# Splitting the later weights of an encoder layer early, storing q and k as rows of three parts, and reading one branch from where it was made

## The chip, the cores and the metric

One core of a Trainium2 chip runs the whole layer. The metric is device time in microseconds (us) of one execution. A NeuronCore has five engines, each with an in-order stream of instructions: TensorE (PE, matrix products; PEld is its weight load), VectorE (DVE), ScalarE (ACT), GpSimd (POOL) and SyncE (SP), which here issues nearly all transfers (DMAs). They meet only at semaphores.

## The reference, cut to what matters

```
h = rmsnorm(x, norm_g)                                   # x: 1024 tokens x 1024
q, k, v, glu_a, glu_b, pool_in, sgu_u, sgu_v, gates = split(h @ w_in)   # 8 pieces of 256, gates 1024
y_a = neighborhood_attention(q, k, v, na_rpb)            # 8 heads of 32, windows of 8 rows x 16 columns
y_b = silu(layernorm(depthwise_conv31(glu_a * sigmoid(glu_b)))) @ conv_pw
y_c = pool_scale * grouped_linear(multiscale_mean(pool_in) - pool_in)
y_d = gelu(sgu_u) * (sgu_w applied per chunk of 128 to layernorm(gelu(sgu_v)) + sgu_b)
y   = concat(y_a, y_b, y_c, y_d) * silu(gates)
out = rmsnorm(x + y @ w_out, final_g)
```

All inputs are float32. A big product is made from parts: each operand is split into `hi` (rounded to PE's float32r) and `lo = x - hi`, and three products hi*hi, lo*hi and hi*lo are added in one PSUM bank.

## The kernel before

**Stages.** First h is normalised and split into `hhi` and `hlo` (128 channels x 8 x 1024 tokens), while v and sgu_v are projected (L213, until about 55 us). Then comes the middle stage: the other 20 blocks of 128 output channels, in the order of the list `work`. Items 0 to 3 feed the convolution (glu_b, glu_a twice), 4 and 5 are q and k of the first four heads, 6 and 7 the pooling, 8 and 9 sgu_u, 10 and 11 q and k of the other heads, 12 to 19 the eight gate blocks, for the branch blocks 6, 7, 4, 5, 0, 2, 3, 1 of the concatenation (0 and 1 attention, 2 and 3 convolution, 4 and 5 pooling, 6 and 7 spatial gating). An item is two *banks* (512 tokens each) of 24 matmuls (L371), so there are 40 banks. Last come two halves of the output projection (L822, L856) with the residual and the final norm.

**Weights.** `prep` loads item n+1 (512 KB) when item n begins; ACT rounds each half to `whi` (L354), and `wlo` is made by POOL in two pieces per half for items 0 to 8 (L360), by DVE for items 9 to 19 (L356). `wraw` has two buffers, `whi` and `wlo` three each.

**What runs beside it.** Each bank ends with its `evac_*` function on ACT and DVE. Between banks generators are advanced: `conv_steps` (97 steps, 92 taps on DVE, L584) over banks 4 to 22; `att_steps` (18 steps, from bank 18 to 37), each with scores on PE (L475 to L478), bias and maximum on DVE, a reduction over partitions on POOL (L488), exponentials on ACT and the product with v on PE (L516, sums by L520); and `conv_norm` (5 steps, banks 23 to 27): mean (L612), variance on PE (L622), two small trips through DRAM (`s_d`, L626 to L634) that end in the row `rb`, then swish (L637 to L644) and the pointwise product (L651). After the fourth and the last group of heads the sums of the exponentials also make a trip through DRAM (`o_d`, `r_d`, L526 to L539).

**Through DRAM.** q and k are written to DRAM in parts hi and lo, and gathered per head into `kst` (hi, lo, hi, a mask) and `qst` (hi, hi, lo, a mask), three DMAs of 32 partitions and one for the mask each time. The spatial gating result `ut` goes to `yd_d` and comes back to `yr` when its gate block begins (L675, L722), as pooling does through `yc_d`.

**Order.** The program is written in this order, and a scheduler then sets the order on each engine from its own estimate of times. z banks for the items: two PSUM buffers.

Of the kernel before, what the change touches and what calls it, by code (L numbers as in the profile page):

```python
# [16 lines left out]
P = 128  # L17
D = 1024
# [28 lines left out]
POOL_W = 9  # L47

ATT0, ATT1, CONV0, CONV1 = 18, 37, 4, 22
# [9 lines left out]
def encoder_kernel(ctx: ExitStack, tc: tile.TileContext, a: dict, out: bass.AP):  # L59
# [273 lines left out]
    yr = {kt: slot("yr") for kt in (6, 7, 4, 5)}  # L333
    sq = [slot("sq") for _ in range(2)]
    yb = [slot("yb") for _ in range(2)]
# [11 lines left out]
    def prep(ct, eng):  # L347
        raw = wpool.tile([P, KO, P], F32, name="wraw")
        ld.dma_start(out=raw, in_=a["w_in"][ct])
        wts[ct] = []  # L350
        for q in range(2):
            hi = wpool.tile([P, 4, P], F32R, name="whi", bufs=3)
            lo = wpool.tile([P, 4, P], F32R, name="wlo", bufs=3)
            s.activation(out=hi, in_=raw[:, 4 * q:4 * q + 4], func=AF.Copy)  # L354
            if eng is v:
                v.tensor_tensor(out=lo, in0=raw[:, 4 * q:4 * q + 4], in1=hi, op=ALU.subtract)  # L356
# [20 lines left out]
    q_d = dram.tile([2, 2, 4, DH, S], F32, name="q_d")  # L377
    k_d = dram.tile([2, 2, 4, DH, SW], F32, name="k_d")
# [3 lines left out]
    def evac_q(hg):  # L382
        hi, lo = qkt[hg][0:2]

        def f(b, z):
# [42 lines left out]
    def att_loads(gi):  # L428
# [177 lines left out]
    def conv_norm():  # L606
        for b in range(2):
# [27 lines left out]
        yield  # L635
        for c in range(2):
            v.tensor_tensor(out=cc[c][:, 0:S], in0=cc[c][:, 0:S], in1=rb, op=ALU.mult)  # L637

        for c in range(2):
            t = sq[c][:, 0:S]  # L640
            s.activation(out=cc[c][:, 0:S], in_=cc[c][:, 0:S], func=AF.Identity, scale=cvec[:, 1, c:c + 1],
                         bias=cvec[:, 2, c:c + 1])
            s.activation(out=t, in_=cc[c][:, 0:S], func=AF.Tanh, scale=0.5)
            v.scalar_tensor_tensor(out=cc[c][:, 0:S], in0=t, scalar=1.0, in1=cc[c][:, 0:S], op0=ALU.add, op1=ALU.mult)  # L644
        yield
        for c in range(2):
            for b in range(2):
                sl = slice(b * 512, (b + 1) * 512)
                ps = bbank()
                for k in range(2):  # L650
                    pe.matmul(ps, lhsT=pw[:, k, c * P:(c + 1) * P], rhs=cc[k][:, sl], start=(k == 0), stop=(k == 1))  # L651
                s.activation(out=yb[c][:, 0:S].rearrange("p (n e) -> p n e", e=2)[:, :, b], in_=ps, func=AF.Copy, scale=0.5)
            yield


    yd_d = dram.tile([2, P, S], F32, name="yd_d")

    def evac_u(c):
        u = ut[c]

        def f(b, z):
# [12 lines left out]
            if b == 1:  # L674
                ld.dma_start(out=yd_d[c], in_=u[:, 0:S])  # L675
# [38 lines left out]
    y = {0: ya[0], 1: ya[1], 2: yb[0], 3: yb[1]}  # L714
    y.update(yr)

    def evac_g(kt, src):
        def f(b, z):
            br = y[kt]
            sl = slice(b * 512, (b + 1) * 512)  # L720
            if b == 0 and src is not None:
                ld.dma_start(out=br[:, 0:S], in_=src)  # L722
# [3 lines left out]
            if src is not None:  # L726
# [8 lines left out]
    for c in range(2):  # L735
# [3 lines left out]
    work += [(T_G + kt, evac_g(kt, src)) for kt, src in  # L739
             ((6, yd_d[0]), (7, yd_d[1]), (4, yc_d[0]), (5, yc_d[1]), (0, None), (2, None), (3, None), (1, None))]  # L740
# [4 lines left out]
    att, conv, norm = att_steps(), conv_steps(), conv_norm()  # L745
    prep(work[0][0], g)
    bank = 0
    for n, (ct, evac) in enumerate(work):
        if n + 1 < len(work):
            prep(work[n + 1][0], g if n + 1 < POOL_W else v)  # L750

        for b in ((1, 0) if n == 0 else (0, 1)):
# [4 lines left out]
            for gen, count, b0, b1 in ((att, 18, ATT0, ATT1), (conv, 97, CONV0, CONV1), (norm, 5, CONV1 + 1, CONV1 + 5)):  # L757
# [16 lines left out]
    def wo_pair(j, half, hi, lo):  # L774
        raw = wpool.tile([P, 2, 512], F32, name="wraw")
# [181 lines left out]
```

## Time and profile before

| | us |
|---|---|
| median of 3 runs | 436.57 (436.07 to 437.01) |
| profiled execution | 435.86 |
| its span, first to last instruction | 434.1 |
| PE busy in the span | 415.9 (96%) |
| DVE, ACT, POOL busy | 312.3, 184.8, 112.2 |
| mean granted PE clock | 0.985 of full speed |

The span is 1.76 us shorter than the execution's own time. PE is busy nearly all of it, so time can come only from the 18.2 us in which it is not, or from those in which it runs at a lower clock.

### The profile page before, as it was taken

What the parts mean: (1) busy time and instruction counts of PE and PEld (TensorE: products, weight loads), DVE (VectorE), ACT (ScalarE), POOL (GpSimd) and SP (SyncE); (2) the same over time, 40 slices, a digit from 0 to 9 for tenths busy, and PEclk for the clock granted to TensorE, in tenths of its full rate; (3) what the DMA queues carried; (4) which work ended last, traced back from release to release, by engine and by line L of the source; (5) the groups of instructions that cost most, each with busy time, mean ns of one, the idle gap of its engine ahead of it and who ended that gap; (6) DMA issues with size and microseconds to landing.
All of it is one profiled execution on the core that took longest, in us unless ns stands there. A gap on an engine that the chain in (4) does not pass through costs nothing.

```text
span 434.1 us, 5888 instructions
## 1 busy us (share of the span) xinstructions
PE 415.9 (96%) x2150; PEld 331.2 (76%) x2150; DVE 312.3 (72%) x540; ACT 184.8 (43%) x314; POOL 112.2 (26%) x90
## 2 busy tenths in 40 slices
PE   7899999999999999999978889999999999999994
PEld 6788878888888778777846647787787788888883
DVE  4798676888988799999798647997882580093332
ACT  6757655222232328334336733344342452254332
POOL 0763402322226821111111101221111243620000
PEclk9999999999999999999995999999999999999998
DMA  7995106311775124163893141522011384402222
GB/s 273 421 418 186 54 25 206 88 48 51 228 245 150 48 97 146 50 219 104 271 235 90 52 168 54 170 94 65 11 48 61 122 269 183 145 2 97 97 98 97
DMA packets 28294, 59.56 MB, mean 137 GB/s; under 512 B 3910, under 2 KB 13354, under 8 KB 28266
## 3 DMA queue, kind: packets, MB, share of 16 engines
q1 hardware_dynamic: 28122, 58.93, 40.9%
q8 instruction: 17, 0.28, 0.3%
q10 hardware_dynamic: 144, 0.26, 0.2%
q14 instruction: 11, 0.09, 0.1%
HBM read 46.71 MB, written 12.47 MB: 136 GB/s over the span
## 4 chain that ended last, share of the span: by engine, by line
PE 80%; DMA 9%; DVE 5%; SPq 2%; ACT 1%; issue 1%; POOL 1%; DVEq 0%; ACTq 0%; POOLq 0%
PE z_ps L371 45%; DMA yr<-yd_d 3%; PE sb L213 3%; PE z_ps L213 3%; PE sb L822 3%; PE sb L856 3%; PE z_ps L822 2%; PE b_ps L856 2%; PE z_ps L856 2%; DMA xT_sb<-in_xT_dram 2%; PE pv L516 2%; PE sa L822 1%; PE ac L213 1%; PE b_ps L822 1%; PE pv L822 1%; PE ac L822 1%
## 5 line engine op out<-in xcount | busy, mean ns | idle before, releaser
L371 PE MATMUL z_ps<-hhi,whi 128*128 128x512 f32 x320 | 90.0, 400 | 1.5 <-DVE yr L728 1.3
L371 PE MATMUL z_ps<-hlo,whi 128*128 128x512 f32 x320 | 89.6, 398 | 0.0
L371 PE MATMUL z_ps<-hhi,wlo 128*128 128x512 f32 x320 | 87.8, 395 | 0.0
L371 PEld LDWEIGHTS z_ps<-hhi,whi 128*128 128x128 f32 x320 | 59.3, 190 | 17.8 <-issue 3.0
L371 PEld LDWEIGHTS z_ps<-hlo,whi 128*128 128x128 f32 x320 | 60.3, 189 | 14.8 <-issue 2.5
L371 PEld LDWEIGHTS z_ps<-hhi,wlo 128*128 128x128 f32 x320 | 60.5, 190 | 13.8 <-issue 1.1
L488 POOL PARTITION_ALL_REDUCE R<-M x16 | 29.9, 1868 | 134.3 <-DVE M L509 128.9
L584 DVE SCALAR_TENSOR_TENSOR ac<-d,pk,ac 128x512 f32<-128x512 f32 x62 | 46.6, 751 | 2.6 <-ACT ac L596 0.9
L360 POOL TENSOR_TENSOR wlo<-wraw,whi 128x256 fp32r<-128x256 f32 x36 | 27.4, 784 | 68.6 <-ACT whi L354 68.6
L354 ACT ACTIVATE whi<-wraw 128x512 fp32r<-128x512 f32 x40 | 25.0, 627 | 33.3 <-PE z_ps L371 31.5
L500 ACT ACTIVATE T<-T 128x1280 f32<-128x1280 f32 x16 | 20.4, 1272 | 15.5 <-DVE T L499 15.5
L584 DVE SCALAR_TENSOR_TENSOR ac<-ch,dws,ac 128x512 f32<-128x512 f32 x30 | 22.6, 755 | 1.8 <-ACT ac L585 0.8
L831 ACT ACTIVATE jk<-res 128x512 f32<-128x512 f32 (+1 forms) x17 | 10.2, 604 | 26.6 <-DVE res L829 25.6
L356 DVE TENSOR_TENSOR wlo<-wraw,whi 128x512 fp32r<-128x512 f32 x22 | 16.8, 764 | 5.1 <-ACT whi L354 5.0
L781 POOL TENSOR_TENSOR wlo<-wraw,whi 128x512 fp32r<-128x512 f32 x8 | 12.1, 1524 | 31.7 <-ACT whi L780 18.9
L829 DVE SCALAR_TENSOR_TENSOR res<-sa,res 128x512 f32<-128x512 f32 x2 | 1.4, 686 | 22.6 <-PE sa L822 22.6
L725 ACT ACTIVATE sg<-z_ps 128x512 f32<-128x512 f32 x16 | 9.5, 596 | 15.5 <-PE z_ps L371 14.1
L499 DVE TENSOR_TENSOR T<-T,pv 128x768 f32<-128x768 f32 x16 | 15.2, 948 | 0.0
L483 DVE SCALAR_TENSOR_TENSOR T<-sb,bt 128x768 f32<-128x768 f32 x16 | 15.2, 948 | 0.0
L505 DVE TENSOR_TENSOR R<-T 128x512 f32<-128x512 f32 x16 | 13.2, 827 | 2.6 <-ACT T L500 2.6
L481 DVE SCALAR_TENSOR_TENSOR T<-sa,bt 128x512 f32<-128x512 f32 x16 | 11.0, 685 | 3.7 <-PE pv L516 2.4
L781 POOL TENSOR_TENSOR wl<-wraw,wh 128x512 fp32r<-128x512 f32 x8 | 10.2, 1294 | 11.3 <-ACT wh L780 11.3
(279 smaller groups left out, 821.6 us busy)
## 6 DMA issues: line engine op xcount, KB each, us to landing
wraw<-in_w_in_dram SPq DMA_DIRECT2D x20, 512.0 KB
res<-in_x_dram SPq DMA_DIRECT2D x8, 512.0 KB
wraw<-in_w_out_dram SPq DMA_DIRECT2D x8, 512.0 KB
out_dram<-res SPq DMA_DIRECT2D x15, 256.0 KB
kst<-k_d SPq DMA_DIRECT2D x24, 136.0 KB
xT_sb<-in_xT_dram SPq DMA_DIRECT2D x6, 512.0 KB
qst<-q_d SPq DMA_DIRECT2D x24, 128.0 KB
vk<-va_d SPq DMA_DIRECT2D x8, 256.0 KB
```

The lines of the kernel that those rows point to most:

```text
L213: pe.matmul(z, lhsT=ha[:, 2 * c + k, ts], rhs=wa[:, k, :], start=(c == 0 and n == 0 and k == 0), stop=(c == 3 and n == 2 and k == 1))
L354: s.activation(out=hi, in_=raw[:, 4 * q:4 * q + 4], func=AF.Copy)
L356: v.tensor_tensor(out=lo, in0=raw[:, 4 * q:4 * q + 4], in1=hi, op=ALU.subtract)
L360: g.tensor_tensor(out=lo[:, w:w + 2], in0=raw[:, 4 * q + w:4 * q + w + 2], in1=hi[:, w:w + 2], op=ALU.subtract)
L371: pe.matmul(z, lhsT=wa[:, k, :], rhs=ha[:, 4 * q + k, b * 512:(b + 1) * 512], start=(n == 0), stop=(n == 3 * KO - 1))
L483: v.scalar_tensor_tensor(out=T[:, :, 256:640], in0=sb[:, :, 0:384], scalar=DH ** -0.5, in1=mf, op0=ALU.mult, op1=ALU.add)
L488: g.partition_all_reduce(R.rearrange("p h x -> p (h x)"), M.rearrange("p h x -> p (h x)"), P, bass.bass_isa.ReduceOp.max)
L500: s.activation(out=T, in_=T, func=AF.Exp)
L584: v.scalar_tensor_tensor(out=ac, in0=src, scalar=w, in1=ac, op0=ALU.mult, op1=ALU.add)
L781: g.tensor_tensor(out=lo[q], in0=raw[:, q], in1=hi[q], op=ALU.subtract)
L822: pe.matmul(acc[t], lhsT=y_[kt][:, ts], rhs=w_[q], start=(j == 0 and q == 0 and n == 0), stop=(j == 3 and q == 1 and n == 2))
L856: pe.matmul(o[:, c0:c1], lhsT=y_[kt][:, ts], rhs=w_[j][:, q, c0:c1], start=(j == 0 and q == 0 and n == 0), stop=(j == 3 and q == 1 and n = ...
```

## The change

1. Items 9 to 19: their weights are loaded and split in banks 1 to 13 by a new generator `split_ahead` (ACT rounds, POOL subtracts, in the buffers that later hold the keys), and both parts are stored in DRAM (`w_d`). `prep` of these items then only loads: hi into `wraw`, lo in two halves into a `whi` and a `wlo` buffer. No `wlo` is made on DVE any more in the middle stage.
2. q and k lie in DRAM as three parts per channel, so that one DMA of 96 partitions fills `qst` or `kst`; the keys' mask rows are loaded once. q and k are each written with three DMAs, before with two.
3. The spatial gating result is gated in place in `ut`; `yd_d` is gone. Pooling's result is loaded two items ahead.
4. The convolution's taps end one bank earlier (21), and its norm has 13 steps over banks 22 to 33; `yb` shares the buffers `sq`.
5. Banks 25, 28, 31 and 34 use the PSUM bank `ac` of the convolution in place of one of the two z buffers. The first half block of w_out is loaded into a query buffer, and its lo part made by DVE.

```diff
-POOL_W = 9
-ATT0, ATT1, CONV0, CONV1 = 18, 37, 4, 22
+NOW = 9
+EARLY0, EARLY1 = 1, 13
+ATT0, ATT1, CONV0, CONV1, NORM1 = 18, 37, 4, 21, 33
...
+    def prep(n):
+        ct = work[n][0]
+        wts[ct] = []
+        raw = wpool.tile([P, KO, P], F32 if n < NOW else F32R, name="wraw")
+        if n < NOW:
+            ld.dma_start(out=raw, in_=a["w_in"][ct])
+        else:
+            ld.dma_start(out=raw.bitcast(F32), in_=w_d[n][0])
...
+            else:
+                hi = part
+                lo = wpool.tile([P, 4, P], F32R, name=("whi", "wlo")[q], bufs=3)
+                ld.dma_start(out=lo.bitcast(F32), in_=w_d[n][1][:, 4 * q:4 * q + 4])
...
+    def split_ahead():
+        for n in range(NOW, len(work)):
+            w_d[n] = [dram.tile([P, KO, P], F32, name=f"w_d{n}_{i}") for i in range(2)]
+            raw = at.tile([P, 1280], F32, name="T", bufs=3)[:, 0:D].rearrange("p (k c) -> p k c", k=KO)
+            hi, lo = (ktile(2 * (n % 2) + i)[:, 0:D].rearrange("p (k c) -> p k c", k=KO) for i in range(2))
+            ld.dma_start(out=raw, in_=a["w_in"][work[n][0]])
+            for q in range(2):
+                ks = slice(4 * q, 4 * q + 4)
+                s.activation(out=hi[:, ks], in_=raw[:, ks], func=AF.Copy)
+                low(lo[:, ks], raw[:, ks], hi[:, ks])
+                if q == 1:
+                    for d, t in zip(w_d[n], (hi, lo)):
+                        ld.dma_start(out=d, in_=t.bitcast(F32))
+                yield
...
-        z = zbank()
+        z = pso.tile([P, 512], F32, name="ac") if CONV1 < bank < ATT1 - 1 and bank % 3 == 0 else zbank()
...
-        for c, n in enumerate((0, 1, 0)):
-            ld.dma_start(out=kst[hg, h][32 * c:32 * c + 32].bitcast(F32), in_=k_d[hg, n, h])
-        ld.dma_start(out=kst[hg, h][96:128].bitcast(F32), in_=kc_d)
+        kst[hg, h] = ktile(h)
+        ld.dma_start(out=kst[hg, h][0:96].bitcast(F32),
+                     in_=k_d[hg, DH * h:DH * h + DH].rearrange("d n x -> (d n) x"))
+        if hg == 0:
+            ld.dma_start(out=kst[hg, h][96:128].bitcast(F32), in_=kc_d)
...
-            if b == 1:
-                ld.dma_start(out=yd_d[c], in_=u[:, 0:S])
...
-            if b == 0 and src is not None:
-                ld.dma_start(out=br[:, 0:S], in_=src)
...
-            for gen, count, b0, b1 in ((att, 18, ATT0, ATT1), (conv, 97, CONV0, CONV1), (norm, 5, CONV1 + 1, CONV1 + 5)):
+            for gen, count, b0, b1 in ((ahead, 2 * (len(work) - NOW), EARLY0, EARLY1), (att, 18, ATT0, ATT1),
+                                       (conv, 97, CONV0, CONV1), (norm, 13, CONV1 + 1, NORM1)):
...
-            g.tensor_tensor(out=lo[q], in0=raw[:, q], in1=hi[q], op=ALU.subtract)
+            (v if (j, half) == (0, 0) else g).tensor_tensor(out=lo[q], in0=raw[:, q], in1=hi[q], op=ALU.subtract)
```

Three places show how the built programs differ. The first is SP's queue around the norm's trips through DRAM, before: `yr<-yd_d` are the two loads of the spatial gating result, `wraw` the weight load of the item after next, `s_d` and `cr` the norm's small trips, `sq<-s_d` its row.

```order
L440 DMA qst<-q_d 32x4x256 x3
L441 DMA qst<-qm_d 32x1024
L432 DMA vk<-va_d 128x4x128
L722 DMA yr<-yd_d 128x1024
L626 DMA s_d<-sg 4x256
L628 DMA cr<-s_d 128x8
L526 DMA o_d<-sg 4x256
...
L632 DMA s_d<-cr 128x8
L634 DMA sq<-s_d 128x1024
L349 DMA wraw<-in_w_in_dram 128x1024
L432 DMA vk<-va_d 128x4x128
L722 DMA yr<-yd_d 128x1024
```

The same place in the changed program; the buffer numbers tell which item a `w_d` belongs to (964 is item 14, 1109 item 16, 1052 item 15).

```order
L664 DMA s_d<-sg 4x256
L361 DMA wraw<-w_d_0_964 128x1024
L563 DMA o_d<-sg 4x256
L666 DMA cr<-s_d 128x8
L372 DMA whi<-w_d_1_1109 128x512
L372 DMA wlo<-w_d_1_1109 128x512
L361 DMA wraw<-w_d_0_1052 128x1024
L670 DMA s_d<-cr 128x8
L476 DMA qst<-q_d 96x4x256
L478 DMA qst<-qm_d 32x1024
L471 DMA vk<-va_d 128x4x128
L672 DMA sq<-s_d 128x1024
```

Both loads of `yr` from `yd_d` are gone, and the norm's second write to DRAM (L670) now stands behind three loads of stored weights, each of which waits for PE to have read its buffer for the last time.

The second place is DVE at the norm's end, before: L637 and L644 are the norm, L356 the lo part of a weight, L727 and L728 the gating of the spatial gating block.

```order
L637 TENSOR_TENSOR cc<-cc,sq 128x1024 x2
L644 SCALAR_TENSOR_TENSOR cc<-sq,cc 128x1024
L356 TENSOR_TENSOR wlo<-wraw,whi 128x512
L644 SCALAR_TENSOR_TENSOR cc<-sq,cc 128x1024
L356 TENSOR_TENSOR wlo<-wraw,whi 128x512
L727 TENSOR_TENSOR z_ps<-z_ps,yr 128x512 x2
```

The same place in the changed program, from the last gating of a spatial gating block (L761, L762 on `ac`) on; L570 is the reciprocal of the attention's sums, L518 and L520 the bias of a score step.

```order
L761 TENSOR_TENSOR ac<-ac,u 128x512
L762 SCALAR_TENSOR_TENSOR u<-sg,ac 128x512
L534 TENSOR_TENSOR T<-T,pv 128x2x256
L536 TENSOR_TENSOR T<-T,pv 128x2x384
L676 TENSOR_TENSOR cc<-cc,sq 128x1024 x2
L570 RECIPROCAL den<-den 128x32
...
L518 SCALAR_TENSOR_TENSOR T<-sa,bt 128x2x256
L520 SCALAR_TENSOR_TENSOR T<-sb,bt 128x2x384
L684 SCALAR_TENSOR_TENSOR cc<-sq,cc 128x1024 x2
```

The spatial gating blocks are gated ahead of the norm's multiplication, and between that and the swish DVE now has the reciprocal, a gate block and one score step.

The third place is PE at the end of the middle stage, before: after the last product with v (L516, L520) 18 matmuls of the output projection (L822) and then the last two banks, of which the first row is shown.

```order
L520 MATMUL pv<-R,ones 32x256 x4
L822 MATMUL sa<-whi,yhi 128x512
L822 MATMUL sb<-whi,yhi 128x512
L822 MATMUL ac<-whi,yhi 128x512
L822 MATMUL b_ps<-whi,yhi 128x512
...
L822 MATMUL pv<-whi,ylo 128x512
L371 MATMUL z_ps<-hhi,whi 128x512 x4
```

The same place in the changed program.

```order
L557 MATMUL pv<-R,ones 32x256 x4
L863 MATMUL pv<-whi,yhi 128x512
L863 MATMUL pv<-wlo,yhi 128x512
L863 MATMUL pv<-whi,ylo 128x512
L409 MATMUL z_ps<-hhi,wraw 128x512 x4
```

Three matmuls of the output projection are left there; the other 15 now stand ahead of the last product with v.

## Rows read from the trace of the kernel before

**Rows 1.** The page: what each engine did, and GB/s in 40 slices.
```profile
PE 415.9 (96%) x2150; PEld 331.2 (76%) x2150; DVE 312.3 (72%) x540; ACT 184.8 (43%) x314; POOL 112.2 (26%) x90
GB/s 273 421 418 186 54 25 206 88 48 51 228 245 150 48 97 146 50 219 104 271 235 90 52 168 54 170 94 65 11 48 61 122 269 183 145 2 97 97 98 97
```

**Rows 2.** Windows: length, busy us (count) of five engines, granted clock, DMA share, GB/s.
```profile
60.00:145.00 85.00, 85.00 (x375) 70.04 (x374) 68.89 (x132) 26.33 (x43) 28.86 (x35) 1.00 0.44 136
170.00:210.00 40.00, 40.00 (x291) 31.40 (x291) 39.25 (x68) 15.93 (x24) 5.88 (x3) 1.00 0.43 146
210.00:270.00 60.00, 52.81 (x275) 36.52 (x274) 43.87 (x67) 28.91 (x41) 9.45 (x5) 0.91 0.48 136
```

**Rows 3.** The same columns, for ten of these 60 us.
```profile
230.00:240.00 10.00, 8.68 (x29) 6.83 (x29) 8.14 (x15) 7.39 (x10) 2.88 (x2) 0.67 0.31 85
```

**Rows 4.** The chain that ended last: start, us, what.
```profile
61.12 84.34 PE z_ps L371 x372
...
224.21 6.28 DMA yr<-yd_d
...
236.56 1.43 DMA s_d<-cr
...
238.06 3.78 DMA sq<-s_d
...
249.20 4.95 DMA yr<-yd_d
```

**Rows 5.** Timeline of PE: start, us, what, count, idle time ahead and its releaser.
```profile
227.54 1.08 PE L622 MATMUL b_ps<-sq,mean_w 128*32 128x256 f32 x8
...
232.06 2.07 PE L371 MATMUL z_ps<-hhi,whi 128*128 128x512 f32 x4 [1.32 <-DVE yr L728]
...
247.85 1.10 PE L651 MATMUL b_ps<-cc,pk 128*128 128x512 f32 x2 [0.80 <-DVE cc L644]
```

**Rows 6.** Timeline of SP, the transfers' issues.
```profile
221.39 1.43 SPq L440 DMA_DIRECT2D qst<-q_d  x3
...
224.21 1.50 SPq L722 DMA_DIRECT2D yr<-yd_d  x1
...
248.34 0.34 SPq L349 DMA_DIRECT2D wraw<-in_w_in_dram  x1
```

**Rows 7.** Waits of SP between 205 and 260 us: total, times, longest.
```profile
SPq L349 <- DVE wlo L356: 10.5, 2, 9.9
```

**Rows 8.** Groups on DVE between 170 and 280 us.
```profile
L356 DVE TENSOR_TENSOR wlo<-wraw,whi 128x512 fp32r<-128x512 f32 x11 | 7.5, 685 | 0.8 <-ACT whi L354 0.7
...
L727 DVE TENSOR_TENSOR z_ps<-z_ps,yr 128x512 f32<-128x512 f32 x6 | 4.1, 696 | 4.9 <-DMA yr<-yd_d 4.9
```

**Rows 9.** POOL's line 360: ns min/median/max, first and last start.
```profile
L360 POOL TENSOR_TENSOR wlo<-wraw,whi x36: 731/740/1263, 38.0 to 141.5; 128x256 fp32r<-128x256 f32 x36
```

**Rows 10.** Timeline of ACT, the last work ahead of the new splits.
```profile
78.23 0.83 ACT L585 ACTIVATE ac<-ch,pk,dws 128x512 f32<-128x512 f32 x1
```

**Rows 11.** Windows, columns as in the second group.
```profile
70.00:90.00 20.00, 20.00 (x90) 16.53 (x89) 14.56 (x23) 6.51 (x9) 6.19 (x8) 1.00 0.42 129
90.00:110.00 20.00, 20.00 (x90) 16.57 (x89) 16.46 (x29) 4.18 (x7) 5.34 (x8) 1.00 0.11 37
110.00:130.00 20.00, 20.00 (x90) 16.57 (x89) 17.62 (x28) 6.42 (x12) 4.36 (x7) 1.00 0.79 254
```

**Rows 12.** Timeline at the end of the middle stage.
```profile
327.45 0.61 PE L520 MATMUL pv<-R,ones 128*32 128x256 f32 x8
...
339.32 1.29 DVE L539 TENSOR_TENSOR ya<-ya,T 128x512 f32<-128x512 f32 x2 [5.29 <-DMA T<-r_d]
340.53 0.68 DVE L730 SCALAR_TENSOR_TENSOR sg<-sg,z_ps 128x512 f32<-128x512 f32 x1
...
344.67 0.50 PE L822 MATMUL z_ps<-whi,yhi 128*128 128x512 f32 x1 [0.73 <-DVE sg L730]
```

More of the change, by code (lines that the diff above doesn't have):

```diff
@@ L332, in encoder_kernel @@
     ya += [slot("ya") for _ in range(2)]
-    yr = {kt: slot("yr") for kt in (6, 7, 4, 5)}
+    yr = {kt: slot("yr") for kt in (4, 5)}
     sq = [slot("sq") for _ in range(2)]
-    yb = [slot("yb") for _ in range(2)]
+    yb = sq
     wts = {}
@@ L345, in bias_rows, with low @@
                 s.activation(out=bt[:, :, m, r, :], in_=bt[:, :, 0, r, :], func=AF.Identity, bias=rowm[:, m, r:r + 1])
-    def prep(ct, eng):
-        raw = wpool.tile([P, KO, P], F32, name="wraw")
-        ld.dma_start(out=raw, in_=a["w_in"][ct])
-        wts[ct] = []
-        for q in range(2):
[L352 to L356, printed above, removed]
-            else:
-                for w in range(0, 4, 2):
-                    g.tensor_tensor(out=lo[:, w:w + 2], in0=raw[:, 4 * q + w:4 * q + w + 2], in1=hi[:, w:w + 2],
-                                    op=ALU.subtract)
+    def low(lo, raw, hi):
+        for w in range(0, 4, 2):
+            g.tensor_tensor(out=lo[:, w:w + 2], in0=raw[:, w:w + 2], in1=hi[:, w:w + 2], op=ALU.subtract)
@@ new lines, in prep @@
+    def prep(n):
+        ct = work[n][0]
+        wts[ct] = []
+        raw = wpool.tile([P, KO, P], F32 if n < NOW else F32R, name="wraw")
[3 more added lines that the diff above has]
+            ld.dma_start(out=raw.bitcast(F32), in_=w_d[n][0])
+        for q in range(2):
+            part = raw[:, 4 * q:4 * q + 4]
+            if n < NOW:
+                hi = wpool.tile([P, 4, P], F32R, name="whi", bufs=3)
+                lo = wpool.tile([P, 4, P], F32R, name="wlo", bufs=3)
+                s.activation(out=hi, in_=part, func=AF.Copy)
+                low(lo, part, hi)
+            else:
+                hi = part
+                lo = wpool.tile([P, 4, P], F32R, name=("whi", "wlo")[q], bufs=3)
+                ld.dma_start(out=lo.bitcast(F32), in_=w_d[n][1][:, 4 * q:4 * q + 4])
@@ L362, in prep, with ktile @@
             wts[ct].append((hi, lo))
+    kbuf = {}
+    def ktile(h):
+        if h not in kbuf:
+            kbuf[h] = at.tile([P, SW], F32R, name=f"kst{h}", bufs=1)
+        return kbuf[h]
+    w_d = {}
+    def split_ahead():
[12 more added lines that the diff above has]
+                yield
@@ L614, in conv_norm @@
                 v.tensor_tensor(out=cc[c][:, sl], in0=cc[c][:, sl], in1=mu, op=ALU.subtract)
+            yield
         for c in range(2):
@@ L720, in f @@
             sl = slice(b * 512, (b + 1) * 512)
-            if b == 0 and src is not None:
-                ld.dma_start(out=br[:, 0:S], in_=src)
             sg = at.tile([P, 512], F32, name="sg")
             s.activation(out=sg, in_=z, func=AF.Tanh, scale=0.5)
-            if src is not None:
+            if early:
                 v.tensor_tensor(out=z, in0=z, in1=br[:, sl], op=ALU.mult)
@@ L738, in encoder_kernel @@
     work += [(T_U, evac_u(0)), (T_U + 1, evac_u(1)), (T_Q + 1, evac_q(1)), (T_K + 1, evac_k(1))]
[L739 to L740 removed]
+    work += [(T_G + kt, evac_g(kt, n < 4)) for n, kt in enumerate((6, 7, 4, 5, 0, 2, 3, 1))]
+    back = {T_G + kt: (yr[kt], yc_d[kt - 4]) for kt in (4, 5)}
     def done(bank, count, b0, b1):
         return 0 if bank < b0 else -(-count * (min(bank, b1) - b0 + 1) // (b1 - b0 + 1))
[L745 to L746 removed]
+    att, conv, norm, ahead = att_steps(), conv_steps(), conv_norm(), split_ahead()
+    prep(0)
     bank = 0
@@ L749, in encoder_kernel @@
         if n + 1 < len(work):
-            prep(work[n + 1][0], g if n + 1 < POOL_W else v)
+            prep(n + 1)
+        if n + 2 < len(work) and work[n + 2][0] in back:
+            dst, src = back[work[n + 2][0]]
+            ld.dma_start(out=dst[:, 0:S], in_=src)
         for b in ((1, 0) if n == 0 else (0, 1)):
@@ L774, in wo_pair @@
     def wo_pair(j, half, hi, lo):
-        raw = wpool.tile([P, 2, 512], F32, name="wraw")
+        raw = (at.tile([P, 4, 256], F32, name="qst").rearrange("p h x -> p (h x)").rearrange("p (q n) -> p q n", q=2)
+               if (j, half) == (0, 0) else wpool.tile([P, 2, 512], F32, name="wraw"))
         kt = korder[2 * j]
```

40 lines of the change are left out of this document (19 added, 21 removed).

## The prediction

> **What bounds the kernel now.** I read the page first: PE is busy 415.9 us, no other engine comes near [rows 1]. The windows then say where it is held up. From 60 to 145 us and from 170 to 210 us PE is busy every microsecond at full clock; from 210 to 270 us it is busy 52.81 of 60 us, at a granted clock of 0.91 [rows 2]. So that stretch is the kernel's only wide hole. Its price: 60.00 - 52.81 = 7.2 us idle, and (1 - 0.91) x 60 = 5.4 us of clock, together **12.6 us**. The clock part belongs to the hole: it stands at 0.67 between 230 and 240 us [rows 3], between the levels of 1.2 and 2.4 GHz, just behind the first idle piece, and is full elsewhere in these windows.
>
> Next the chain of waits and the timelines of PE and SP, to see what ends last there. SP issues the first return of the spatial gating result at 224.21 us, behind key and query loads [rows 6]. It lands 6.28 us later [rows 4]; DVE stands in front of it, and PE waits for the z bank that DVE should have emptied: 1.32 us ahead of the matmul at 232.06 us [rows 5]. Then the norm: variance on PE at 227.54 us, trips through DRAM that end with the row's 3.78 us [rows 4], swish, and the pointwise product at 247.85 us, where PE waits for DVE [rows 5]. Nothing of weight stands between the two on PE but two banks. The second return is issued at 249.20 us and takes 4.95 us [rows 4]. It was held too: the weight load right ahead of it is issued at 248.34 us [rows 6], SP having stood up to 9.9 us for the `wlo` that DVE had not yet subtracted [rows 7]. DVE idles 4.9 us for these two returns in all [rows 8]. So three things make the hole: returns from DRAM that queue on SP, weight splits in DVE's queue, and a norm whose product is placed on PE too early.
>
> **The change part by part.**
>
> *Spatial gating stays on chip.* Both returns go, with the waits they cause. DVE's gating needs then only the bank itself. Cost nothing; gain within the 12.6 us.
>
> *Weights split early.* DVE loses 11 subtractions of 685 ns between 170 and 280 us, 7.5 us [rows 8], and SP no longer waits for DVE before a weight load. POOL gains 11 x 4 = 44 pieces at a median of 740 ns [rows 9], 32.6 us, in banks 1 to 13. It has room: in 70 to 130 us it is busy 6.19 + 5.34 + 4.36 of 60 us [rows 11]. But POOL works in order, and eight of the new pieces stand ahead of the lo part of item 3's second half. They can begin when ACT has rounded the first half, some 1.2 us after 79.06 us [rows 10], so they end near 80.3 + 8 x 0.74 = 86.2 us and that lo part near 87.7 us. PE, at 0.2267 us a matmul (84.34 / 372, [rows 4]), comes to it after 160 matmuls of the 372 that begin at 61.12 us (item 3 starts behind 3 x 48 = 144, less the 24 done before that row, and its second half needs lo after 16 more): 61.12 + 136 x 0.2267 = 91.9 us. That cover is 4 us; if it goes, PE waits microsecond for microsecond. The later items have more. I take 0.
>
> *Stored weights.* Each item's hi part (512 KB) can only be loaded when PE has ended the item two before, where the old load waited for the split alone. It has one item to land: 48 x 0.2267 = 10.9 us. The nearest rows are the 512 KB returns above, 6.28 and 4.95 us [rows 4], so 4.6 us are left at the worse. I take 0.
>
> By the Trainium skill's page "DMA: Bandwidth & Descriptors" (section "Anatomy of one DMA") a transfer costs about 2.0 us plus its bytes over 436 GB/s, fitted for the GpSimd path. That would be 3.2 us for such a part, an estimate from that page, and would leave 7.7 us; the rows, taken on a loaded queue, say twice as much, and I go by them.
>
> *q and k in three parts, one DMA in place of three.* 24 + 24 loads become 8 + 8, with four more writes. SP issues three query loads in 1.43 us [rows 6], so it gains some 0.9 us a group, on a queue that nobody waits for once the returns are gone. I take 0.
>
> *The norm.* From the variance's end, 227.54 + 1.08 = 228.62 us, to the product at 247.85 us it takes 19.2 us now [rows 5]. In the changed order 118 item matmuls stand between the two on PE, 26.8 us, with attention besides. But the second write to DRAM now stands on SP behind the load of item 15's hi part, and that waits for the end of item 13: 53 matmuls behind the variance, 12.0 us, where the write could go after 236.56 - 228.62 = 7.9 us [rows 4]. The norm becomes 4.1 us longer, 23.3 us, still 3.5 us inside its cover. After that DVE has the reciprocal of the sums, one gate block and a score step ahead of the swish, so a late neighbour costs at once. Bounds: 0, and the longest stand of SP at one weight load, 9.9 us [rows 7], less 3.5, that is 6.4 us. The order covers it and only its neighbours can spoil that, so I take a value near the lower end, **1.5 us**.
>
> *A third bank buffer and the early taps.* They let PE run up to three banks ahead of DVE; the taps end earlier because DVE is rid of the splits in that stretch. No price of their own: this is what lets the hole close.
>
> *The end of the middle stage.* The last product with v ends at 327.45 + 0.61 = 328.06 us, the last trip of the sums gives `ya` at 340.61 us, and the first bank of the last item is read by 341.21 us: 13.1 us [rows 12]. Before, 66 matmuls (18 of the output projection, 48 of the items) covered that with 15.0 us, and PE lost only 0.73 us. Now 51 are left, 11.6 us: PE waits 13.1 - 11.6 = 1.5 us for the first z bank. DVE takes two more steps of 0.68 us until the second is read, of which PE's three matmuls on the first cover 0.7: another 0.7 us. Cost 2.2 - 0.7 = **1.5 us**. Lower bound 0 (if DVE takes the pieces otherwise), upper 3.
>
> **Sum**, against the profiled execution's 435.86 us (0.7 us under the median of the runs, 436.57): 435.86 - 12.6 + 1.5 + 1.5 = **426.3 us**.
>
> **The rivals.**
>
> *The early split starves the front* (chance 0.14). POOL's cover is 4 us, and DMA is the reason to doubt it. The splits add 11 x 1.57 MB = 17.3 MB (one load, two stores each) between some 76 and 130 us, onto 129, 37 and 254 GB/s in the three windows [rows 11], which is 2.6 + 0.7 + 5.1 = 8.4 MB; 25.7 MB in 54 us are 476 GB/s, over the 421 GB/s of the fullest slice [rows 1]. The excess would take 25.7 / 0.421 = 61 us, 7 us late, 3 to 4 us past the cover. Against it: the splits are paced by PE's banks through ACT's order, and the weight loads of items 9 to 19 leave the later stretch. Price 4 us: 430.
>
> *The hole only moves* (0.08). Attention and the norm stay serial on DVE, which is busy 39.25 of 40 us before the hole [rows 2]. If only the removed 7.5 us of splits [rows 8] come off, less the part already idle (4.9 us, [rows 8]), the gain is 2.6 us: 433.
>
> *Slower: stored weights come late* (0.06). SP is one queue, and each hi load waits for PE at its head. If another wait stands there for more than the 4.6 us of cover, the item starts late, and so for each of 11 items. It decides at 12.6 / 11 = 1.15 us of lateness an item, that is at 5.8 us. The 9.9 us of [rows 7] show that SP can stand so long; against it, that wait was for DVE, and PE's last read lies a whole item ahead. At 1.7 us late an item: 426.3 + 18.7 = 445.
>
> *It does nothing that counts* (0.04): PE idles for the attention's own chain of score, maximum and exponential, in the same hole: 436.
>
> **How the numbers follow.** The forecast case has 0.68, with 421.5 to 429 as its own range: below, both costs at 0 give 423.3 and the small idle piece of 0.73 us [rows 12] and its like may close; above, the norm costs 4.5. The range for 8 in 10 reaches on over the first two rivals: **421.5 to 434**. Faster takes the forecast and the first two rivals, less some of their tails: 0.88; same 0.04; slower 0.08. I count as same what lies within 0.2%, 0.9 us, about what a measurement of this kernel tells from no change.
>
> **What would show it.** Right: PE busy nearly all of 210 to 270 us at full clock; no DVE wait for a branch's return; the pointwise product's idle below 2 us; PE's wait at the output projection's first z bank near 1.5 us. Wrong: idle PE between 85 and 130 us, released by POOL (the first rival); PE waiting for a `wraw`, `whi` or `wlo` transfer after 155 us (the third); DVE waiting several microseconds for the norm's row or the sums, with PE behind it (the norm's term, or the second). I would be wrong most of all if SP's order, set from estimated times, holds a transfer that PE needs behind one that waits for PE.

## The result and the profile after

The changed kernel takes **423.36 us** (423.01 to 423.54, 4 runs) beside 436.32 us before: a ratio of 0.970 (95% interval 0.9685 to 0.9718), 13.0 us faster. The forecast was 426.3 us. The profiled execution takes 423.49 us, its span 421.7 us.

The page of the changed kernel, as in [rows 1]:

```profile
PE 410.0 (97%) x2150; PEld 328.2 (78%) x2150; DVE 298.0 (71%) x520; ACT 182.7 (43%) x312; POOL 139.0 (33%) x132
...
GB/s 265 420 419 188 95 31 184 299 354 410 365 409 384 258 294 120 164 140 212 210 291 244 209 146 86 113 113 114 52 0 82 175 309 138 100 2 100 99 101 99
```

PE is busy 5.9 us less with the same 2150 matmuls, and idle 421.7 - 410.0 = 11.7 us in place of 434.1 - 415.9 = 18.2: the first part is nearly all clock (5.4 us in the hole, [rows 2]), the second is waits. Its windows, columns as in [rows 2] and [rows 3]:

```profile
60.00:145.00 85.00, 85.00 (x375) 70.04 (x374) 72.24 (x137) 37.87 (x64) 56.73 (x75) 1.00 0.86 321
170.00:210.00 40.00, 40.00 (x296) 30.84 (x296) 38.88 (x66) 15.33 (x23) 9.46 (x5) 1.00 0.53 172
210.00:270.00 60.00, 60.00 (x367) 45.21 (x365) 43.36 (x69) 25.78 (x36) 8.92 (x5) 1.00 0.65 196
```

```profile
230.00:240.00 10.00, 10.00 (x78) 7.49 (x78) 6.89 (x14) 6.27 (x9) 1.78 (x1) 1.00 0.61 159
```

The hole is gone: 60.00 of 60 us busy at a granted clock of 1.00, where it was 52.81 us at 0.91. PE's timeline shows no idle time between 60 and 318 us. What is left stands at the end of the middle stage (the pointwise product of the norm is the first row):

```profile
253.52 1.02 PE L690 MATMUL b_ps<-cc,pk 128*128 128x512 f32 x2
...
318.50 0.50 PE L863 MATMUL pv<-whi,yhi 128*128 128x512 f32 x1 [0.78 <-ACT sg L562]
...
319.71 0.50 PE L409 MATMUL z_ps<-hhi,wraw 128*128 128x512 f32 x1 [0.25 <-DVE sg L764]
...
332.61 0.50 PE L863 MATMUL z_ps<-whi,yhi 128*128 128x512 f32 x1 [1.01 <-DVE sg L764]
```

The three waits make 0.78 + 0.25 + 1.01 = 2.0 us, in place of the 0.73 us of [rows 12]. The 1.01 us stand at the second z bank of the output projection; at the first, PE arrives at 330.72 us and waits for nothing. DVE in the same stretches, the norm's multiplication and swish first:

```profile
243.82 2.36 DVE L676 TENSOR_TENSOR cc<-cc,sq 128x1024 f32<-128x1024 f32 x2 [1.42 <-DMA sq<-s_d]
...
249.89 2.35 DVE L684 SCALAR_TENSOR_TENSOR cc<-sq,cc 128x1024 f32<-128x1024 f32 x2
...
328.68 1.29 DVE L576 TENSOR_TENSOR ya<-ya,T 128x512 f32<-128x512 f32 x2 [4.98 <-DMA T<-r_d]
```

DVE still waits 1.42 us for the norm's row, but the swish ends at 249.89 + 2.35 = 252.24 us and the product starts at 253.52: nobody waits behind it. The last of these rows is the trip of the sums that sets the 1.01 us above.

### The profile page after: what moved, and what is told of

It is laid out like the page before. It is cut to its first block, busy times and chain, and to the rows that moved or that the text cites. A ratio compares the mean times of both kernels' runs of the same rounds, so it can differ in the third digit from the quotient of the medians.

```text
span 421.7 us, 5959 instructions
## 1 busy us (share of the span) xinstructions
PE 410.0 (97%) x2150; PEld 328.2 (78%) x2150; DVE 298.0 (71%) x520; ACT 182.7 (43%) x312; POOL 139.0 (33%) x132
## 4 chain that ended last, share of the span: by engine, by line
PE 89%; DMA 4%; DVE 2%; SPq 1%; ACT 1%; POOL 1%; issue 0%; ACTq 0%; POOLq 0%
PE z_ps L409 44%; PE ac L409 5%; PE sb L863 3%; PE sb L215 3%; PE z_ps L215 3%; PE sb L897 3%; PE pv L553 3%; PE z_ps L863 2%; DMA xT_sb<-in_xT_dram 2%; PE b_ps L897 2%; PE z_ps L897 2%; PE b_ps L690 2%; PE sa L863 1%; PE pv L557 1%; PE ac L215 1%; PE pv L897 1%
## 5 line engine op out<-in xcount | busy, mean ns | idle before, releaser
L409 PE MATMUL z_ps<-hhi,whi 128*128 128x512 f32 x216 | 59.5, 396 | 0.0
L409 PE MATMUL z_ps<-hhi,wlo 128*128 128x512 f32 x216 | 59.4, 393 | 0.0
L409 PEld LDWEIGHTS z_ps<-hhi,wlo 128*128 128x128 f32 x216 | 40.4, 188 | 9.7 <-issue 1.5
L409 PE MATMUL z_ps<-hhi,wraw 128*128 128x512 f32 x144 | 43.1, 408 | 0.3 <-DVE sg L764 0.3
L409 PE MATMUL z_ps<-hlo,wraw 128*128 128x512 f32 x144 | 39.9, 394 | 0.0
L409 PE MATMUL z_ps<-hlo,whi 128*128 128x512 f32 x144 | 38.6, 389 | 0.0
L352 POOL TENSOR_TENSOR kst<-T,kst 128x256 fp32r<-128x256 f32 x44 | 31.6, 752 | 1.9 <-ACT kst L394 1.8
L409 PEld LDWEIGHTS z_ps<-hhi,wraw 128*128 128x128 f32 x144 | 26.1, 188 | 7.7 <-issue 2.4
L409 PEld LDWEIGHTS z_ps<-hlo,wraw 128*128 128x128 f32 x144 | 26.5, 188 | 6.4 <-issue 1.2
L409 PEld LDWEIGHTS z_ps<-hlo,whi 128*128 128x128 f32 x144 | 27.0, 188 | 5.6
L872 ACT ACTIVATE jk<-res 128x512 f32<-128x512 f32 (+1 forms) x17 | 10.3, 604 | 27.8 <-DVE res L870 26.8
L518 DVE SCALAR_TENSOR_TENSOR T<-sa,bt 128x512 f32<-128x512 f32 x16 | 11.0, 685 | 14.8 <-PE pv L553 12.4
L822 POOL TENSOR_TENSOR wlo<-wraw,whi 128x512 fp32r<-128x512 f32 x6 | 8.3, 1391 | 32.0 <-PE z_ps L409 21.3
```

The lines of the kernel that those rows point to most:

```text
L352: g.tensor_tensor(out=lo[:, w:w + 2], in0=raw[:, w:w + 2], in1=hi[:, w:w + 2], op=ALU.subtract)
L518: v.scalar_tensor_tensor(out=T[:, :, 0:256], in0=sa, scalar=DH ** -0.5, in1=mf[:, :, 64:320], op0=ALU.mult, op1=ALU.add)
```

## The experiments

Twelve runs: five undo one part of the change each (one of them twice), one is the changed kernel again, one splits a transfer, one merges some, and three put one part into the kernel before. Where no other is named, ratios are to the kernel before on the same chip. A caution for all of them: the scheduler sets the order on every engine anew for each edit, so a run measures an edit together with the order that comes with it.

**Undo the spatial gating part.** Spatial gating goes to DRAM and comes back when its gate block begins.

```diff
-    y = {..., 6: ut[0], 7: ut[1]}
+            if b == 1:
+                ld.dma_start(out=yd_d[c], in_=u[:, 0:S])
...
+            if b == 0 and kt in (6, 7):
+                ld.dma_start(out=br[:, 0:S], in_=yd_d[kt - 6])
```

> The changed kernel (423.4 us), but the spatial gating result goes to DRAM again and comes back when its gate block begins. Theory (three causes make the hole together): two returns of 5 to 6 us again stand between PE's bank and DVE, PE waits 1 to 3 us for the z bank in 215 to 260 us: 425 to 429 us. Rival (the splits in DVE's queue alone made the hole, the returns are hidden once DVE is free and there is a third bank): 423 to 424 us, no PE wait in that stretch.

Measured 422.03 us (421.34 to 422.17), ratio 0.9663 (0.9636 to 0.9691): not slower, but 1.3 us below the changed kernel. The theory's 425 to 429 falls. Both were run again on one chip:

> The changed kernel itself, beside the variant of it that brings the spatial gating result back from DRAM, on one chip. If that variant's 422.0 us were only another chip, this kernel comes out within 0.3 us of it; if the order that the return brings is better by itself, this kernel stands 1 to 2 us above it: 423 to 424 us.

> The variant with the spatial gating result brought back from DRAM, once more, beside the changed kernel on the same chip. If it is better by itself: 421.5 to 422.5 us and below the changed kernel by 1 to 2 us. If the first difference was the chip's: within 0.3 us of it.

Measured 423.61 us (423.33 to 423.83) for the changed kernel and 421.77 us (421.03 to 422.62) for the variant. The two ranges don't meet, so the variant is the better kernel, by 1.8 us. Why is not settled: the hole stays closed in both (60.00 and 59.41 of 60 us busy). The first trace of the variant has 1.8 us less busy time of PE for the same matmuls (408.2 against 410.0 us), but in the second pair of traces it is 0.4 us (409.3 against 409.7), and no single wait accounts for the rest.

**Undo the early split.** The splits are made in the middle stage again, by DVE from item 9 on.

```diff
-NOW = 9
+NOW = 20
+POOL_W = 9
...
+        if n >= POOL_W:
+            v.tensor_tensor(out=lo, in0=raw, in1=hi, op=ALU.subtract)
+            return
```

> The changed kernel, but items 9 to 19 are split when they are used, by ACT and DVE as before the change; nothing is stored in DRAM. Theory (three causes together): DVE has 7.5 us more work between 170 and 280 us, SP waits for DVE's lo part again, and part of the hole is back: 426 to 432 us. Rival (the splits alone made the hole): the whole hole is back, 434 to 436 us. Second rival (the splits lie beside PE's work; the norm and the returns made the hole): 423 to 424.5 us, and the early split was not needed.

**Undo the norm's steps.** Taps to bank 22, the norm in 5 steps over banks 23 to 27 (the rule of the third bank keeps its banks).

```diff
-ATT0, ATT1, CONV0, CONV1, NORM1 = 18, 37, 4, 21, 33
+ATT0, ATT1, CONV0, CONV1, NORM1 = 18, 37, 4, 22, 27
...
-(norm, 13, CONV1 + 1, NORM1)
+(norm, 5, CONV1 + 1, NORM1)
```

> The changed kernel, but the convolution's taps end at bank 22 and its norm has 5 steps over banks 23 to 27, as before the change. Theory (three causes together): the pointwise product stands on PE ahead of what DVE can deliver, PE idles there and the clock drops behind it: 426 to 431 us, with a window of clock below 1.00 in 220 to 260 us. Rival (the splits alone made the hole): 423 to 424 us.

**Undo the third bank.** All items use the two z buffers.

```diff
-        z = pso.tile([P, 512], F32, name="ac") if CONV1 < bank < ATT1 - 1 and bank % 3 == 0 else zbank()
+        z = zbank()
```

> The changed kernel, but all items use the two z banks; the convolution's bank is not lent. Theory: the third bank takes up DVE's bursts of 3 to 5 us (norm steps of 2.4 us, score steps); without it PE waits for a z bank several times between 210 and 300 us, 1 to 4 us in all: 424.5 to 428 us. Rival (DVE is never a bank late once the splits and the returns are gone): 423 to 424 us.

Measured 430.58 us (429.07 to 432.0; ratio 0.9862, 0.982 to 0.9904), 429.63 us (428.53 to 430.24; 0.9838, 0.9805 to 0.987) and 429.96 us (429.46 to 431.09; 0.9856, 0.9819 to 0.9892). Beside 423.36 us they cost 7.2, 6.3 and 6.6 us; the first two are inside the theory's ranges, the bank is 2 us beyond its own. The rivals, the splits alone and a hole that is gone without the third bank, fall. But a time inside a range is not yet the mechanism. The windows of the three kernels, in this order, show where the loss lies:

```profile
210.00:270.00 60.00, 60.00 (x343) 45.49 (x341) 51.50 (x79) 29.86 (x41) 12.44 (x6) 1.00 0.44 129
290.00:310.00 20.00, 15.11 (x122) 11.13 (x115) 18.21 (x29) 8.60 (x15) 4.18 (x3) 0.79 0.13 41
```

```profile
220.00:240.00 20.00, 17.83 (x128) 14.48 (x127) 15.07 (x26) 10.90 (x16) 3.56 (x2) 1.00 0.84 247
290.00:310.00 20.00, 17.15 (x136) 12.29 (x135) 15.31 (x25) 6.40 (x11) 3.56 (x2) 0.91 0.15 46
```

```profile
220.00:240.00 20.00, 16.33 (x112) 12.51 (x101) 14.68 (x24) 9.13 (x13) 3.57 (x2) 0.91 0.66 181
290.00:310.00 20.00, 20.00 (x127) 15.97 (x126) 14.71 (x25) 6.51 (x10) 3.83 (x2) 1.00 0.25 74
```

With the splits on DVE the hole does not come back where it was, between 170 and 280 us; it opens at 290 to 310 us, 4.9 us idle at a clock of 0.79 with DVE busy 18.21 of 20 us. DVE's extra work (51.50 us busy from 210 to 270 us, in place of 43.36) turns into waits of PE only later.

The norm in five steps costs 2.2 us at 220 to 240 and 2.9 us later, but not by the theory's mechanism: PE never waits at the pointwise product (L687, from 254.13 us), and the clock is 1.00 from 210 to 290 us. PE's waits there are for score steps on DVE (1.00 + 0.29 us) and for a spatial gating block (0.87 us).

Without the third bank the first hole opens again, but PE's waits for a z bank between 210 and 300 us make 0.2 us, not the theory's 1 to 4. Half of the hole is not DVE's doing. PE's timeline in that kernel, from the score step of the second group's third and fourth heads on:

```profile
223.80 0.33 PE L512 MATMUL sa<-qst,kst 128*128 128x128 f32 x1 [0.70 <-DVE T L518]
...
226.13 0.33 PE L512 MATMUL sa<-qst,kst 128*128 128x128 f32 x1 [1.90 <-DMA kst<-k_d]
```

In the changed kernel the 24 matmuls of an item in the third bank stand ahead of the same step:

```profile
228.93 1.07 PE L409 MATMUL ac<-hhi,wraw 128*128 128x512 f32 x4
...
234.37 0.22 PE L512 MATMUL sa<-qst,kst 128*128 128x128 f32 x1
```

PE waits for the keys of the second group of heads, and these were not loaded later: SP issues them from 215.98 us, in the changed kernel from 216.44. PE comes to them earlier, with no bank of an item in between. This wait stood in no term of the forecast.

**Undo the layout of q and k.** Two parts, three loads of 32 partitions per buffer, as before.

```diff
-        ld.dma_start(out=kst[hg, h][0:96].bitcast(F32),
-                     in_=k_d[hg, DH * h:DH * h + DH].rearrange("d n x -> (d n) x"))
+        for c, n in enumerate((0, 1, 0)):
+            ld.dma_start(out=kst[hg, h][32 * c:32 * c + 32].bitcast(F32), in_=k_d[hg, n, h])
...
```

> The changed kernel, but q and k lie in DRAM in two parts as before, three DMAs of 32 partitions per buffer and no more rows repeated. Forecast's reading (SP has time once nobody waits for its returns): 423 to 424.5 us. Rival (the issues of the many small loads stand ahead of loads that PE needs: 24 + 24 in place of 8 + 8, some 0.5 us each): PE waits for keys or queries between 205 and 230 us, 425 to 429 us.

Measured 434.70 us (433.39 to 436.08), ratio 0.9964 (0.9949 to 0.998): 11.1 us over the changed kernel on the same chip. The forecast's reading falls, and the rival's range is 6 us too low. This one part undone takes nearly the whole gain. Timeline of SP with it undone, the key loads:

```profile
211.34 2.64 SPq L486 DMA_DIRECT2D kst<-k_d  x6
...
218.56 1.25 SPq L486 DMA_DIRECT2D kst<-k_d  x3
...
221.26 0.96 SPq L486 DMA_DIRECT2D kst<-k_d  x2
...
222.80 1.33 SPq L486 DMA_DIRECT2D kst<-k_d  x1
```

The same of the changed kernel:

```profile
214.03 0.79 SPq L483 DMA_DIRECT2D kst<-k_d  x2
...
216.44 0.80 SPq L483 DMA_DIRECT2D kst<-k_d  x2
```

And PE with it undone:

```profile
231.43 0.30 PE L514 MATMUL sa<-qst,kst 128*128 128x128 f32 x1 [1.52 <-DMA kst<-k_d]
...
235.02 2.07 PE L409 MATMUL ac<-hhi,wraw 128*128 128x512 f32 x4 [2.71 <-DVE u L764]
```

The last key load is issued after 222.8 us, 6 us later than in the changed kernel, and PE waits for it until 231.43. The second wait, 2.71 us, is for DVE, and the chain of this kernel says where that comes from:

```profile
221.26 7.83 DMA kst<-k_d
...
229.15 3.34 DMA s_d<-sg
...
232.57 0.39 ACT sg L564
...
233.05 0.61 ACT pv L535
...
233.68 0.69 DVE T L536
234.37 0.61 DVE u L764
```

A key load ends, only then does SP issue the norm's first write (`s_d`), ACT gets the buffer `sg` back when that has landed, and DVE is let go by ACT. The clock is 0.67 in the window from 230 to 240 us. The write has nothing to do with the keys. The built program says why it waits for them. Its transfers on SP use eight semaphores in turn, and each waits until the one eight places ahead has landed; in this run's program the first write is place 180 and a key load place 172. Nine consecutive places in the changed program:

```
147 L788 DMA yr<-yc_d 128x1024 [waits DMAHW3_49]
148 L483 DMA kst_722<-k_d 96x1088 [waits DMAHW4_49,PE_49]
149 L483 DMA kst_723<-k_d 96x1088 [waits PE_49]
150 L476 DMA qst<-q_d 96x4x256
151 L478 DMA qst<-qm_d 32x1024
152 L372 DMA whi<-w_d_1_1053 128x512 [waits DMAHW0_49]
153 L471 DMA vk<-va_d 128x4x128 [waits DMAHW1_49,PE_49]
154 L372 DMA wlo<-w_d_1_1053 128x512 [waits DMAHW2_49,PE_49]
155 L664 DMA s_d<-sg 4x256 [waits DMAHW3_49,Activation_49]
```

The norm's sums (place 155) have nothing to do with the pooling block (place 147), and yet SP's waits in the trace of the changed kernel say:

```profile
SPq L664 <- DMA yr<-yc_d: 1.1, 1, 1.1
```

With the old layout SP's waits of this kind are longer, at the load of a mask and at the norm's first write:

```profile
SPq L480 <- DMA yr<-yc_d: 2.0, 1, 2.0
SPq L666 <- DMA kst<-k_d: 0.5, 1, 0.5
```

So the number of transfers can count on this queue, beside their bytes. How much of PE's loss it makes is not shown by these rows: the score step that waits for the keys also stands on PE ahead of the third bank's matmuls again (the row at 235.02), as in the run without that bank. The next run keeps layout and bytes and edits the number of transfers alone.

```diff
-        ld.dma_start(out=kst[hg, h][0:96].bitcast(F32),
-                     in_=k_d[hg, DH * h:DH * h + DH].rearrange("d n x -> (d n) x"))
+        rows = k_d[hg, DH * h:DH * h + DH].rearrange("d n x -> (d n) x")
+        for c in range(3):
+            ld.dma_start(out=kst[hg, h][32 * c:32 * c + 32].bitcast(F32), in_=rows[32 * c:32 * c + 32])
...
```

> The changed kernel with q and k in DRAM as rows of three parts, but each buffer of queries or keys filled by three transfers of 32 partitions in place of one of 96: the same layout and bytes, 24 + 24 transfers in place of 8 + 8. Theory (the number of transfers counts: a transfer in the program waits for the one eight places ahead of it in the queue, so small ones hold up all that is behind them): most of the loss of the run with the old layout comes back, 429 to 435 us, and PE waits for a key buffer between 220 and 235 us. Rival (the layout or the extra copy of a part in DRAM counts): 423 to 425 us.

Measured 442.91 us (440.55 to 444.27), ratio 1.0132 (1.0106 to 1.0159): the direction is the theory's, the size is 8 us beyond it, and the rival (layout or the third copy) falls. PE does not wait for a key buffer between 220 and 235 us, as the theory had it. Its long wait is a later one:

```profile
240.87 0.48 PE L515 MATMUL sa<-qst,kst 128*128 128x128 f32 x1 [6.62 <-DMA vk<-va_d]
```

The releaser in this row is only the event that came last. This matmul reads no `vk`, and the built program lets it wait for its queries and for DVE to have read `sa`. The chain of this kernel shows what DVE was held by:

```profile
229.60 2.84 DMA s_d<-cr
...
232.51 5.32 DMA sq<-s_d
...
237.85 2.36 DVE cc L679 x2
240.21 0.60 DVE T L521
```

The row of the norm lands at 232.51 + 5.32 = 237.83 us. That is not late: in the changed kernel DVE gets it only for 243.82 us, after a wait of 1.42 us. But here DVE, which takes its work in order, stands 8.5 us in front of the norm's multiplication (L679), and the reading of the scores (L521), for which PE waits, is behind it. So the largest piece of this loss comes with the order on DVE, and the run does not show how much the number of transfers makes by itself; the 19.3 us over the changed kernel (423.61 us, on another chip) are number and order together.

**One part in the kernel before.** The diffs are the change's own lines for that part (the bank rule; the layout with one load per buffer; the gating in place). The first text below counts banks from 0: they are those of the change, 25, 28, 31 and 34.

> The kernel before, with one edit: banks 24, 27, 30 and 33 take the convolution's PSUM bank in place of a z bank. If the third bank is the main part of the gain by itself: 428 to 431 us. Theory (it only pays once DVE is less than a bank behind on the whole; in this kernel the returns from DRAM and the splits hold DVE longer than one bank): 433 to 436.5 us.

> The kernel before with the new layout of q and k and one transfer per buffer, nothing else (mask rows of the keys loaded each time as before). If the many key and query loads made the hole: 427 to 431 us. If each of the other parts (splits on DVE, five-step norm) holds the hole open by itself, as the runs that undo them let one think: 433 to 437 us.

> The kernel before with the spatial gating result gated where it was made, nothing else. Forecast's reading (the two returns of 6.3 and 5.0 us on the chain are a cause of the hole): 429 to 434 us. Rival (they stand on the chain only because the queue is late there already; what is next in it takes their place): 435 to 438 us.

Measured 442.06 us (440.74 to 443.48; ratio 1.0139, 1.0108 to 1.0171), 436.16 us (434.92 to 437.22; 0.9994, 0.998 to 1.0008) and 433.06 us (432.35 to 433.5; 0.9923, 0.991 to 0.9936). The third bank alone makes the kernel 5.9 us slower, which neither theory had: from 210 to 270 us PE is busy 52.77 of 60 us at a clock of 0.91, as without it, and the loss comes behind that, with 6.05 us idle between 270 and 345 us in place of 1.07. The layout alone does nothing. The gating alone gains 3.2 us (55.09 of 60 us busy at 0.94). The returns from DRAM were on the path of the kernel before, as the forecast read, for a quarter of the hole. The row of its chain ahead of the first return of [rows 4] shows what that stood behind:

```profile
219.94 4.26 DMA kst<-k_d
```

It is a key load too; SP issued the return when it had landed. In that kernel's program the return is place 138 and the key load place 130, eight ahead.

**Fewer transfers for the sums.** From the variant with the return put back (421.8 us).

```diff
-        for h in range(4):
-            ld.dma_start(out=rec[32 * h:32 * h + 32], in_=r_d[hg, h].partition_broadcast(DH))
+        src = r_d[hg]
+        ld.dma_start(out=rec, in_=bass.AP(tensor=src.tensor, offset=src.offset, ap=[[S, 4], [0, DH], [1, S]]))
```

> The variant that brings the spatial gating result back (421.8 us), and the sums of the attention come back in one transfer to 128 partitions in place of four to 32. Theory (three issues of about 0.45 us and a part of the 4.98 us that DVE waits for them go, and PE's waits for the gated sums at the end of the middle stage, about 1.2 us, go with them): 420.3 to 421.3 us. Rival (the landing, not the issue, is what DVE waits for): 421.5 to 422.3 us.

Measured 432.52 us (429.63 to 435.99), ratio 0.9911 (0.9878 to 0.9944): 10.7 us slower than that variant, against both theories. The chain at the end of the middle stage:

```profile
327.66 8.82 DMA T<-r_d
336.48 0.02 issue
336.51 1.29 DVE ya L576 x2
```

and the same place with four transfers, SP and then DVE:

```profile
323.86 1.71 SPq L573 DMA_DIRECT2D T<-r_d  x4
```

```profile
327.99 1.29 DVE L576 TENSOR_TENSOR ya<-ya,T 128x512 f32<-128x512 f32 x2 [5.03 <-DMA T<-r_d]
```

Four transfers land 327.99 - 323.86 = 4.1 us after the first issue; one with the same 512 KB takes 8.82 us, and PE waits 4.6 us for the bank behind it. DMA's busy share in tenths, in 40 slices from 328.5 to 336.3 us, is what it took:

```profile
DMA  0091111122232223222322232223111215895667
```

With four transfers it was this, in 40 slices from 324.0 to 327.9 us:

```profile
DMA  0000000092967999276996631009549312030000
```

Until other loads join at the end, most slices of the single transfer stand at 1 to 3 tenths: it keeps about a quarter of the 16 engines busy. The Trainium skill has this rule, in "DMA: Bandwidth & Descriptors", section "Why a DMA increments its semaphore by 16 and not by 1": a transfer is spread over as many engines (up to 16) as divide the slowest dimension of both its patterns. Here that is the 4 heads, so 4 of 16; the row of the single transfer, with its 1 to 3 tenths, agrees. The trip after the fourth group was merged as well, and PE is busy 8.87 and 8.26 us in the two stretches of 10 us from 250 us on.

## Why the prediction was right, point by point

- **The hole's price.** 12.6 us, from 7.2 us idle and 5.4 us of clock: right. All 60 us are busy at 1.00 now. The forecast read the clock as full outside 230 to 240 us; in the trace of the kernel before it was 0.82 already from 220 to 230 us.
- **The end of the middle stage.** Forecast 1.5 us (2.2 us less the old 0.7); measured 2.0 - 0.73 = 1.3 us. The size is right, and so is the mechanism: from the last product with v (317.10 + 0.61 us) the trip takes until 330.58 us, 12.9 us against the forecast 13.1, and outlasts PE's shorter cover. The place is not: 0.78 + 0.25 us of the waits, for ACT and DVE to empty banks, come inside the trip, where the forecast had none, and so nothing is left to wait for at the first z bank, where it had 1.5.
- **The norm.** Forecast 1.5 us between bounds of 0 and 6.4; measured 0, the lower bound. The term was mis-sized: the chain grew, from variance to swish it is 252.24 - 221.35 = 30.9 us against 19.2 (variance end from 220.54 + 0.81), more than the 23.3 expected, but the product on PE was later too, 253.52 - 221.35 = 32.2 us behind the variance, where the forecast counted 26.8 us of item matmuls and left the attention beside them uncounted. The slack was 253.52 - 252.24 = 1.3 us: covered, only just, by a piece of cover that no term held.
- **The sum.** 435.86 - 12.6 + 1.3 = 424.6 us; the remaining 1.1 us to 423.49 are small idle pieces that closed (0.34 us from 270 to 300 us, 0.4 us in the first 60 us and behind 345 us) and 0.4 us of PE time beyond the clock's 5.4.
- **Stored weights late.** No wait of PE for a `w_d` part after 155 us; SP stood up to 9.4 us for PE at the load of a stored part, and PE waited for nothing behind it.

**The first rival (the front)** did not come, but the cover was thinner than worked out, as these rows of POOL and then of PE show:

```profile
81.65 5.64 POOL L352 TENSOR_TENSOR kst<-T,kst 128x256 fp32r<-128x256 f32 x8 [0.86 <-ACT kst L394]
88.06 1.44 POOL L352 TENSOR_TENSOR wlo<-wraw,whi 128x256 fp32r<-128x256 f32 x2 [0.77 <-ACT whi L367]
```

```profile
91.91 1.07 PE L409 MATMUL z_ps<-hhi,wlo 128*128 128x512 f32 x4
```

Item 3's lo part was done at 89.50 us, not 87.7, and PE came to it at 91.91, as forecast: 2.4 us of cover, not 4. The DMA side was as full as feared:

```profile
90.00:110.00 20.00, 20.00 (x90) 16.57 (x89) 16.54 (x29) 8.69 (x15) 16.71 (x25) 1.00 1.01 392
110.00:130.00 20.00, 20.00 (x90) 16.53 (x90) 18.09 (x28) 9.51 (x19) 15.12 (x22) 1.00 1.00 376
```

PE was busy all 40 us at full clock: the full queue cost it nothing here.

**The step that failed** is the apportioning. "On a queue that nobody waits for once the returns are gone. I take 0": undone, the layout of q and k costs 11.1 us. "No price of their own" for the third bank: 6.6 us undone, and 5.9 us *lost* when it is put alone into the kernel before. "Three things make the hole" with the returns first: PE's wait there was 1.32 us of the 7.2 us idle [rows 5], the return gains 3.2 us when it alone is taken out of the kernel before, and put back into the changed kernel it costs nothing and is even 1.8 us faster. "A norm whose product is placed on PE too early": with the five steps back PE has no wait at that product. What the runs showed in place of it: with any one of four parts undone PE idles again, at several places and for several releasers: the second group's keys, score steps, gating blocks, and steps of ACT. Undone one at a time these four add up to 7.2 + 6.3 + 6.6 + 11.1 = 31.2 us, over twice the gain; the three put alone into the kernel before add up to a loss of 5.9 - 3.2 - 0.1 = 2.6 us. The total was forecast from the hole, and that is why it came out; from a sum over the parts it could not have.

A rival to "all these parts are needed" is not excluded by any run: each edit brings a new order on every engine, and the changed kernel may simply have an order without waits that most edits lose. The score step for the second group's last keys is an example: in two of the runs it stands ahead of a bank's 24 matmuls, in the changed kernel behind them. The run with three loads is another: its norm's row is there 6 us earlier than in the changed kernel, and PE waits 6.62 us all the same.

**Open:** why the variant with the return is 1.8 us faster, why the third bank harms the kernel before, and how much of each part's loss, and of the 19.3 us, is the part itself and how much the order that came with it. A run with the order held fixed would tell, and was not made.

The best kernel here is the changed one with the spatial gating result brought back from DRAM: 421.77 us, ratio 0.9674 (0.9655 to 0.9693).

## What to carry to other kernels

Price a change that closes a hole by the hole, idle time and clock together, and look for what else could keep it open; don't give each part a share, and don't judge a part by undoing it alone or adding it alone. When an undone part costs what was expected, look whether PE waits where it was expected: of three runs here two came inside their ranges, one of them by other waits and one at another place. On a queue whose transfers wait for one another in turn, read the waits of SP for a transfer whose data the waiting one doesn't use (up to 2.0 us here). Where a wait has several possible releasers, look up in the built program which of them it can be. Before merging transfers, look at the slowest dimension of the merged pattern: three loads in place of one of 96 partitions cost 11 and 19 us here, together with the order that came with them; merging four loads into one with 4 outermost cost 10.7.

## What the runs showed of the hardware

- DMA at a busy share of 1.00 for 40 us, at 376 to 392 GB/s, left PE at full clock and without a wait.
- A 512 KB broadcast read took 8.82 us as one transfer with the slowest dimension 4, with a DMA share of 1 to 3 tenths, and 4.1 us as four.
- PE's clock fell again where PE paused: 0.67 in the ten microseconds with 4.1 us of idle time in the run with the old layout, 0.79 in the 20 us with 4.9 us in the run with the splits on DVE.
